# One more row in seven products, later output splits, earlier weights, and the prompt's attention work in unused columns of the score tiles: one step of a two-layer diffusion backbone

## The chip, the cores and the metric

The kernel runs on one core of one Trainium2 chip. A core has TensorE (matrix products; PE in the profile, PEld for its weight loads), VectorE (DVE), ScalarE (ACT), GpSimd (POOL) and SyncE (SP, which here only issues DMAs). Each engine works through its own queue in order and waits for the others through semaphores. Matrix products land in PSUM, which has eight banks of 512 fp32 columns in each of 128 partitions; everything else lives in SBUF. The metric is the device time of one execution in microseconds, as a median of runs.

## The reference

Two streams of tokens pass through two layers with the same weights: 128 prompt tokens, and 512 latent tokens that also see the prompt's cached keys and values. Layer 0 mixes with eight latent-compressed heads (MLA) and eight neighbourhood heads, layer 1 with grouped queries; after each mixer comes a SwiGLU FFN of width 2816. Shift, scale and gate of every sub-layer are made from a condition vector (the modulation).

```python
for l in range(DEPTH):
    sh1_s, sc1_s, g1_s, sh2_s, sc2_s, g2_s = ada_modulation(cond_lat, w_mod[l], b_mod[l])
    hs = modulate(rms_norm(xs, norm_mix[l]), sh1_s, sc1_s)
    out_s = ...          # even: q, k, v of 8 MLA heads, softmax over 512 + 128 keys; neighbourhood heads; @ w_out
    xs = xs + g1_s * out_s
    hs = modulate(rms_norm(xs, norm_ffn[l]), sh2_s, sc2_s)
    xs = xs + g2_s * swiglu(hs, w_ffn_in[l], w_ffn_out[l])
# the same for the prompt's tokens, which read only prompt tokens
def swiglu(h, w_in, w_out):
    gate, up = jnp.split(h @ w_in, 2, axis=-1)
    return (jax.nn.silu(gate) * up) @ w_out
```

## The kernel before

Activations lie with the 1024 features on partitions (8 blocks of 128) and the 640 tokens (512 latent, 128 prompt) on columns, which are worked in two halves of 320 (`HALF`). Products keep fp32 precision by splitting each operand in a high part (a ScalarE copy to fp32r) and a low part (a VectorE subtraction); `mm3` runs three matmuls for one product: high x high, high x low, low x high. Every weight block therefore costs a DMA, a ScalarE pass and a VectorE pass (`unit`, or `load` and `split`).

PSUM has two families of tiles: four banks of kind "m" (`bank`), and four more whose use changes by stage (`open_y`): single banks of kind "y", or in the attention stages two score tiles of two banks each (`bank2`, tag "s"). In a score tile of MLA, `mla_scores` uses columns 0 to 319 of each bank, and columns 320 to 511 lie unused.

Tiles and semaphores are placed by a framework that orders each engine's queue at build time, by the order in which the code writes the operations and by a model of when each becomes ready. `after(inst, fn)` and `run` add an order only: what `fn` issues on the engine of `inst` is queued behind it. `sequence(order, pieces)` runs named pieces in a written order, each behind the last matmul before it.

**MLA heads** (loop over `h` = 0 to 7; `p, r = divmod(h, 2)`, so `r` is 0 for even heads). The pieces of one head in `MLA_ORDER` are: `s0` to `s3`, the scores of four blocks of 128 latent queries against 640 keys (six matmuls into a score tile `ms`, a maximum on VectorE (L963), an exponential on ScalarE (L965), a reciprocal and a scaling on GpSimd); `q0`, `q1`, the queries of the next head; `k0`, `k1`, the keys of the next pair of heads (odd heads only); `sp`, the prompt's scores of this head; and, one head late, `t0` to `t4`, the transposes of the five blocks of probabilities with their split into `mts` (L390, L391), and `v0` to `v4`, their products with the values into `mo`. `v3` and `v4` run another head later under the names `w3` and `w4`. In the first head of a pair come also `pt` and `pv`, the transposes and value products of the prompt's probabilities of the pair before (`prompt_pair`, names mpp). All of q, k, t, mo, sp, pt and pv take banks of kind "m". The neighbourhood heads use `prompt_pair` as well, with their own banks.

**Output splits.** `rsplit` splits the attention outputs for the projection: `oNs` (neighbourhood heads, ready before the MLA heads begin) behind the fourth exponential of heads 0, 2, 4 and 5; `oMs` 0 to 2 (MLA) where the framework finds room after their pair is done, and `oMs` 3 at the end.

**Output projection** (`mixer_out`, name oa in layer 0, oc in layer 1): for each of eight output blocks n, a weight unit and 2 x 8 x 3 matmuls, then the residual (L324) and the norm's sums. From n = 1 on `beside(n - 1)` adds modulation tiles: a DMA `wm` and two VectorE products `junk` (L1630) each, whose sums are the modulation of the FFN's output and of layer 1. `early` (off in layer 0, on in layer 1) makes the weight unit of n ahead of these tiles. In the first two blocks the last operand, oMs3, comes late, so both wait with their last eighth.

**FFN rows** (`ffn`). The 22 blocks of the hidden width are rows. The first `FEW[l]` rows are made whole: gate and up, two halves, 8 blocks, `mm3`. The later rows use a form of seven products of half the depth (`product`, names fg, fd, fu) in place of eight: `seven` builds four weight tiles from the raw pair with four VectorE sums and four splits, and the activations' sums D, N, C, E are made by `add_up` during rows 0 and 1. `split` places its tiles in turn in the pools wp and fp, by the counter `turn`; the output stage's `wout` uses the same counter to choose between the pools rawp/wp and fo. The activations of most rows are spilled to memory and read back for the output stage.

Of the kernel before, what the change touches and what calls it, by code (L numbers as in the profile page):

```python
# [18 lines left out]
P = 128  # L19
D = 1024  # L20
KT = D // P
NS = 512
# [29 lines left out]
def body(ctx, tc, xT, vecs, crow, wm0, wm0g1, wm0g, wm1, wA, wNV, wNA, wMK, wMV, wOA, wGQ, wGK, wGV, wOC,  # L52
# [53 lines left out]
    def f(ap):  # L106
        return ap.bitcast(F32)
# [19 lines left out]
    def named(prefix, pieces):  # L127
        return {f"{prefix}{i}": piece for i, piece in enumerate(pieces)}
# [54 lines left out]
    def mm3(ps, a, b, h, l, st, sp, **k):  # L183
        PE.matmul(ps, a, h, start=st, stop=False, **k)
        PE.matmul(ps, a, l, start=False, stop=False, **k)
        PE.matmul(ps, b, h, start=False, stop=sp, **k)
# [196 lines left out]
        V.reciprocal(r, l)  # L383
        G.tensor_scalar(pt[:, :n], pt[:, :n], r, 0.0, ALU.mult, ALU.add)

    def pt_split(ps, n, pool, name):
        bufs = 5 if pool.name == "cp" else 3
        h = pool.tile([P, 512], F32R, tag="pth", bufs=bufs, name=name + "h")
        l = pool.tile([P, 512], F32R, tag="ptl", bufs=bufs, name=name + "l")
        S.activation(h[:, :n], ps[:, :n], AF.Copy)  # L390
        V.tensor_tensor(l[:, :n], ps[:, :n], f(h[:, :n]), ALU.subtract)  # L391
        return h, l

    def tr(out, in_):
        PE.transpose(out, in_, ident)
# [18 lines left out]
    def prompt_pair(vs, o, pool, name, sbank):  # L414

        pt = pool.tile([P, 256], F32, tag="pp", bufs=1, name=name + "p")

        def first(r, product):
            def run():
                pss = sbank(f"{name}s{r}")[:, :P]  # L420
                product(pss)
                m = tiny.tile([P, 1], F32, tag="m2", name=f"{name}m{r}")
                V.tensor_reduce(m, pss, AX.X, ALU.max, negate=True)
                l = tiny.tile([P, 1], F32, tag="l2", name=f"{name}l{r}")
                sl = pt[:, r * P:(r + 1) * P]
                S.activation(sl, pss, AF.Exp, bias=m, accum_out=l)
                softmax_tail(sl, l, f"{name}r{r}", P)
            return run

        box = []  # L430

        def trs():
            pst = bank(name + "t")
            for r in range(2):
                tr(pst[:, r * P:(r + 1) * P], pt[:, r * P:(r + 1) * P])
            box.extend(pt_split(pst, 256, pool, name + "pt"))

        def av():
            th, tl = box
            pso = bank(name + "o")  # L440
            for r in range(2):
                out = pso[:, r * P:(r + 1) * P]
# [3 lines left out]
            S.activation(t[:, :256], pso[64:128, :256], AF.Copy)  # L446
            for r in range(2):
                V.tensor_tensor(o[64 * r:64 * r + 64, NS:T], pso[0:64, r * P:(r + 1) * P], t[:, r * P:(r + 1) * P], ALU.add)

        return first, {"pt": trs, "pv": av}  # L450

# [378 lines left out]
    def k_tiles(r, p):  # L830
        return odd_keys[p % 2] if r else even_keys
# [118 lines left out]
    def mla_q(h):  # L950
        return q_pieces(h, qbank, lambda c: cp.tile([P, T], F32R, tag=f"mq{c}", bufs=2, name=f"mq{c}{h}"), lambda: tq[:, h % 2, :])

    def mla_scores(h, pts):
        r = h % 2
        ll = tiny.tile([P, 4], F32, tag="ll", bufs=4, name=f"ml{h}")

        def piece(j):
            qh, ql = mqs[h]
            pss = bank2(f"ms{h}_{j}")
            kh, kl = [t[0] for t in k_tiles(r, h // 2)]  # L960
            scores(pss, (qh[:, P * j:P * j + P], ql[:, P * j:P * j + P]), kh, kl)
            nm = tiny.tile([P, 1], F32, tag="nm", name=f"mn{h}_{j}")
            V.tensor_reduce(nm, pss[:, :, :HT], AX.XY, ALU.max, negate=True)  # L963
            pt = cp.tile([P, T], F32, tag="mp", bufs=8, name=f"mp{h}_{j}")
            exps[h, j] = S.activation(halves(pt), pss[:, :, :HT], AF.Exp, bias=nm, accum_out=ll[:, j:j + 1])  # L965
# [31 lines left out]
    for i in range(6):  # L997
        if i not in mvb and i not in BESIDE:
            mv_late(i)
    tail, oM, oNs = {}, [], []  # L1000

    MLA_ORDER = ("s0 w3 q0 w4 s1 t0 t1 pt s2 v0 t2 pv q1 v1 t3 s3 v2 t4 sp",
                 "s0 w3 q0 w4 s1 k0 t0 t1 q1 s2 v0 k1 t2 s3 v1 t3 v2 sp t4")
    late = {}
    for h in range(8):
        p, r = divmod(h, 2)
        if r == 0:
            oM.append(cp.tile([P, T], F32, tag="om", bufs=4, name=f"oM{p}"))
            pfirst, psecond = prompt_pair([mv[5][:, 2 * p + i, :] for i in range(2)], oM[p], cp, f"mpp{p}",
                                         bank)  # L1010
        pts = []
        sc = mla_scores(h, pts)
        qh, ql = mqs[h]
        pieces = named("s", sc)
        pieces["sp"] = pfirst(r, lambda pss, qh=qh, ql=ql, ks=k_tiles(r, p): mm3(pss, qh[:, NS:T], ql[:, NS:T], ks[0][1], ks[1][1], True, True))
# [654 lines left out]
    def x_again(n):  # L1670
# [10 lines left out]
    x, pend = mixer_out(wOA, oMs + oNs, [4, 5, 6, 7, 0, 1, 2, 3], x_again, mods[0], "oa", nxt, op[-1], before(op[1], op[5], (1, 1, 1, 1, 0, 0, 0)))  # L1681
    box2, nxt = next_mod("h10", gs[1][0], mods[1], SH1)
    x, pend = ffn(0, x, pend, box["m"], nxt, side, op)

# [378 lines left out]
```

## Time and profile before

| | |
|---|---|
| median of 3 runs | 1493.82 us (1493.72 to 1495.14) |
| the profiled execution | 1495.92 us |
| its span | 1494.1 us |
| TensorE / VectorE / ScalarE / GpSimd busy | 97% / 83% / 53% / 12% |
| mean granted TensorE clock | 0.994 |
| moved by DMA | 231.48 MB, 155 GB/s |

The page names engines PE, PEld, DVE, ACT, POOL and SP; L64 is a line of the kernel, and as every matmul is issued by one helper, matmuls are told apart by their tiles (out<-in). Matmuls overlap, so that a matmul of 320 columns is shown with about 0.31 us while the next begins earlier; busy time is the union of these. "[0.66 <-DVE x]" behind a row is the idle time of that engine before it and what ended it. In the windows each engine's busy time is followed by its instructions in brackets.

### The profile page before, as it was taken

The page shows a single profiled execution, that of the slowest core. Times are in us where ns is not written, and L with a number is a line of the kernel's source. Part 1 is how long each engine was busy: PE and PEld are TensorE (multiplying, and loading weights), DVE is VectorE, ACT ScalarE, POOL GpSimd, SP SyncE. Part 2 cuts the span into 40 slices and gives each one's busy share as a digit, 9 for nine tenths or more (in the row PEclk, how much of TensorE's full clock was granted, in tenths as well). Part 3 has the DMA queues.
Part 4 walks back from the last instruction along what each step waited for, and adds up shares of the span by engine and source line. Part 5 has one row for each costly group of instructions (what it writes and reads, how often), then busy time and mean ns, then how long its engine had stood idle before and what let it go on. Part 6 is the DMA issues. An engine that isn't in the chain of part 4 may idle for free.

```text
span 1494.1 us, 25843 instructions
## 1 busy us (share of the span) xinstructions
PE 1448.7 (97%) x9766; PEld 1392.5 (93%) x9766; DVE 1235.9 (83%) x2378; ACT 785.7 (53%) x1542; POOL 178.0 (12%) x272
## 2 busy tenths in 40 slices
PE   6999999999999999999999999999999999999997
PEld 4989978889899999999999999989899999999996
DVE  5877778877878888955998888888899989989976
ACT  5446677763745555541222656672665565555443
POOL 0046635420000000000000122220100000000000
PEclk9999999999999999999999999999999999999999
DMA  9643341025154554559765301115154555548561
GB/s 372 207 151 123 114 145 44 15 81 188 42 208 167 166 166 166 163 181 345 234 215 189 96 27 36 37 40 193 57 170 171 190 175 190 174 151 294 184 260 71
DMA packets 79636, 231.48 MB, mean 155 GB/s; under 512 B 8856, under 2 KB 13240, under 8 KB 79128
## 3 DMA queue, kind: packets, MB, share of 16 engines
q1 hardware_dynamic: 77152, 225.43, 44.2%
q10 hardware_dynamic: 1944, 3.48, 0.7%
q8 instruction: 76, 1.25, 0.3%
q0 software_dynamic: 416, 0.93, 0.2%
q14 instruction: 48, 0.39, 0.1%
HBM read 193.15 MB, written 36.66 MB: 154 GB/s over the span
## 4 chain that ended last, share of the span: by engine, by line
PE 77%; DVE 10%; ACT 6%; DMA 4%; issue 2%; POOL 0%; DVEq 0%; ACTq 0%; SPq 0%; POOLq 0%
PE fg L64 19%; PE fd L64 9%; PE fgo L64 5%; PE fu L64 4%; PE gq L64 3%; PE fdo L64 3%; PE fo L64 2%; DVE junk L1630 2%; PE gs L64 2%; PE go L64 2%; PE nk L64 2%; PE nq L64 2%; PE fuo L64 1%; PE gt L68 1%; PE mod L64 1%
## 5 line engine op out<-in xcount | busy, mean ns | idle before, releaser
L1630 DVE SCALAR_TENSOR_TENSOR junk<-wm,cb 128x1024 bf16<-128x1024 f32 x88 | 107.3, 1219 | 1.8 <-DMA wm<-in_wm 1.2
L64 PE MATMUL gq<-h10h,wgq 128*128 128x320 f32 x256 | 65.8, 316 | 0.0
L261 POOL TENSOR_SCALAR h10h<-h10t,gs,mods 128x320 fp32r<-128x320 f32 x4 | 3.1, 786 | 438.2 <-DVE h10t L255 435.9
L1370 ACT ACTIVATE wY<-s 128x1024 fp32r<-128x1024 f32 x37 | 39.2, 1060 | 27.7 <-PE fg L64 24.0
L1898 POOL TENSOR_TENSOR xr<-xw,fn1rs 128x320 f32<-128x320 f32 x2 | 1.7, 866 | 416.9 <-ACT fn1rs L229 416.9
L1370 ACT ACTIVATE wZ<-s 128x1024 fp32r<-128x1024 f32 x37 | 39.1, 1057 | 18.8 <-PE fd L64 16.5
L1479 DVE TENSOR_TENSOR sg<-up,sg 128x640 f32<-128x640 f32 x37 | 30.5, 823 | 20.7 <-ACT sg L1478 19.6
L1371 DVE TENSOR_TENSOR wZ<-s,wZ 128x1024 fp32r<-128x1024 f32 x37 | 45.2, 1222 | 2.8 <-ACT wZ L1370 0.2
L64 PEld LDWEIGHTS gq<-h10h,wgq 128*128 128x128 f32 x256 | 44.9, 189 | 0.6
L1371 DVE TENSOR_TENSOR wY<-s,wY 128x1024 fp32r<-128x1024 f32 x37 | 45.1, 1219 | 0.3
L1478 ACT ACTIVATE sg<-fg 128x320 f32<-128x320 f32 x37 | 16.2, 438 | 48.7 <-PE fg L64 48.7
L64 PE MATMUL fg<-h01q,wgu 128*128 128x320 f32 x192 | 40.3, 316 | 0.9 <-ACT h01q L298 0.5
L1500 ACT ACTIVATE p<-fd 128x320 f32<-128x320 f32 x37 | 16.2, 438 | 46.9 <-PE fd L64 46.9
L64 PE MATMUL gq<-h10l,wgq 128*128 128x320 f32 x128 | 39.4, 308 | 0.0
L1835 ACT ACTIVATE gp<-gs,gb,rq 128x640 f32<-128x640 f32 (+1 forms) x40 | 31.8, 796 | 13.2 <-DVE gb L1834 11.8
L64 PE MATMUL fg<-h11q,wX 128*128 128x320 f32 x228 | 36.7, 309 | 0.0
L64 PE MATMUL fu<-h11q,wX 128*128 128x320 f32 x228 | 36.6, 309 | 0.0
L64 PE MATMUL fd<-h11q,wZ 128*128 128x320 f32 x228 | 36.6, 309 | 0.0
L64 PE MATMUL fg<-h11E,wW 128*128 128x320 f32 x228 | 36.5, 309 | 0.0
L64 PE MATMUL fg<-h11N,wZ 128*128 128x320 f32 x228 | 36.5, 309 | 0.0
L64 PE MATMUL fd<-h11D,wY 128*128 128x320 f32 x228 | 36.4, 308 | 0.0
L64 PE MATMUL fg<-h11C,wY 128*128 128x320 f32 x228 | 36.4, 308 | 0.0
(3425 smaller groups left out, 5331.1 us busy)
## 6 DMA issues: line engine op xcount, KB each, us to landing
wm<-in_wm SPq DMA_DIRECT2D x48, 512.0 KB, 4.3
mraw<-in_wm SPq DMA_DIRECT2D x8, 1024.0 KB, 13.2
mraw<-in_wm SPq DMA_DIRECT2D x16, 512.0 KB, 4.0
wmv<-in_wm0g SPq DMA_DIRECT2D x8, 512.0 KB, 4.3
wm<-in_wm0g SPq DMA_DIRECT2D x8, 512.0 KB, 3.5
ruo<-in_wFO SPq DMA_DIRECT2D x8, 512.0 KB, 4.7
rgo<-in_wFO SPq DMA_DIRECT2D x8, 512.0 KB, 5.9
x<-in_xT SPq DMA_DIRECT2D x8, 320.0 KB, 5.4
```

The lines of the kernel that those rows point to most:

```text
L64: cls.last = nc.tensor.matmul(*a, **k)
L68: cls.last = nc.tensor.transpose(*a, **k)
L261: G.tensor_scalar(h[:, c0:c1], t, self.gsl[:, k, 0:1], self.ml[:, self.sh + k, 0:1], ALU.mult, ALU.add)
L1370: S.activation(h, src, AF.Copy)
L1371: V.tensor_tensor(w_, src, f(h), ALU.subtract)
L1478: last = S.activation(sg[:, 0:HT], g[:, :HT], AF.Silu, scale=-1.0)
L1479: V.tensor_tensor(sg, up, sg, ALU.mult)
L1500: S.activation(p5, b5[:, :HT], AF.Copy)
L1630: V.scalar_tensor_tensor(junk, raw, 1.0, cb[:, c, :], ALU.mult, ALU.mult, accum_out=mods[l][:, j0 + i, c:c + 1])
L1835: gexp[h, j] = S.activation(dst, src, AF.Exp, bias=nb, scale=rq[:, j:j + 1], accum_out=ll[:, j:j + 1])
L1898: G.tensor_tensor(x[k][:, c0:c1], root[1][k], nrm.rs[:, c0:c1], ALU.mult)
```

## The change

Five edits:

1. `FEW` of layer 0 goes from 4 to 3: row 3 of its FFN is made in seven products.
2. `oNs` 3 is split behind the third exponential of head 7 and `oMs` 0 to 2 behind its fourth, on ScalarE's queue.
3. The output projection of layer 0 is called with `early`.
4. In `MLA_ORDER` of even heads `s1` goes ahead of `w4`, and `sp`, `pt` and `pv` leave the order.
5. `sp`, `pt` and `pv` of the MLA heads are run inside a score piece, right behind its six matmuls and ahead of its maximum, into columns 320 to 447 of the score tile's two banks: in even heads `pt` in `s1`, `sp` in `s2` and `pv` in `s3`, in odd heads `sp` in `s3`. Head 7's `sp` and the last pair's `pt` and `pv` stay as they were, with banks of kind "m".

```diff
-    def pt_split(ps, n, pool, name):
+    def pt_split(ps, n, pool, name, shape=None):
...
-        S.activation(h[:, :n], ps[:, :n], AF.Copy)
-        V.tensor_tensor(l[:, :n], ps[:, :n], f(h[:, :n]), ALU.subtract)
+        shape = shape or (lambda t: t[:, :n])
+        ps = shape(ps) if len(ps.shape) == 2 else ps
+        S.activation(shape(h), ps, AF.Copy)
+        V.tensor_tensor(shape(l), ps, f(shape(h)), ALU.subtract)
...
+        def both(t):
+            return t[:, :256].rearrange("p (a b) -> p a b", a=2)
+
         def first(r, product):
-            def run():
-                pss = sbank(f"{name}s{r}")[:, :P]
+            def run(spare=None):
+                pss = sbank(f"{name}s{r}")[:, :P] if spare is None else spare[:, 0]
...
-        def trs():
-            pst = bank(name + "t")
+        def trs(spare=None):
+            pst = both(bank(name + "t")) if spare is None else spare
             for r in range(2):
-                tr(pst[:, r * P:(r + 1) * P], pt[:, r * P:(r + 1) * P])
-            box.extend(pt_split(pst, 256, pool, name + "pt"))
+                tr(pst[:, r], pt[:, r * P:(r + 1) * P])
+            box.extend(pt_split(pst, 256, pool, name + "pt", both))
...
-        def av():
+        def av(spare=None):
             th, tl = box
-            pso = bank(name + "o")
+            pso = both(bank(name + "o")) if spare is None else spare
...
-    def mla_scores(h, pts):
+    def mla_scores(h, pts, beside):
...
             scores(pss, (qh[:, P * j:P * j + P], ql[:, P * j:P * j + P]), kh, kl)
+            if j in beside:
+                beside[j](pss[:, :, HT:HT + P])
...
-    MLA_ORDER = ("s0 w3 q0 w4 s1 t0 t1 pt s2 v0 t2 pv q1 v1 t3 s3 v2 t4 sp",
+    MLA_ORDER = ("s0 w3 q0 s1 w4 t0 t1 s2 v0 t2 q1 v1 t3 s3 v2 t4",
                  "s0 w3 q0 w4 s1 k0 t0 t1 q1 s2 v0 k1 t2 s3 v1 t3 v2 sp t4")
...
-        sc = mla_scores(h, pts)
         qh, ql = mqs[h]
-        pieces = named("s", sc)
-        pieces["sp"] = pfirst(r, lambda pss, ...: mm3(...))
+        beside = {1: tail.pop("pt"), 3: tail.pop("pv")} if h and r == 0 else {}
+        pieces = named("s", mla_scores(h, pts, beside))
+        (pieces if h == 7 else beside)["sp" if h == 7 else 3 - (r == 0)] = pfirst(r, lambda pss, ...: mm3(...))
...
-        if h in (0, 2, 4, 5):
+        if h in (0, 2, 4):
             oNs.append(after(exps[h, 3], lambda: rsplit(oN[len(oNs)], f"oNs{len(oNs)}")))
-    oMs = [rsplit(oM[p], f"oMs{p}") for p in range(3)]
+    oNs.append(after(exps[7, 2], lambda: rsplit(oN[3], "oNs3")))
+    oMs = [after(exps[7, 3], lambda: rsplit(oM[p], f"oMs{p}")) for p in range(3)]
...
-    FEW = 4, 3
+    FEW = 3, 3
...
-    x, pend = mixer_out(wOA, oMs + oNs, ..., before(op[1], op[5], (1, 1, 1, 1, 0, 0, 0)))
+    x, pend = mixer_out(wOA, oMs + oNs, ..., before(op[1], op[5], (1, 1, 1, 1, 0, 0, 0)), True)
```

More of the change, by code (lines that the diff above doesn't have):

```diff
@@ L430, in prompt_pair @@
         box = []
-        def trs():
-            pst = bank(name + "t")
+        def trs(spare=None):
+            pst = both(bank(name + "t")) if spare is None else spare
             for r in range(2):
-                tr(pst[:, r * P:(r + 1) * P], pt[:, r * P:(r + 1) * P])
-            box.extend(pt_split(pst, 256, pool, name + "pt"))
-        def av():
+                tr(pst[:, r], pt[:, r * P:(r + 1) * P])
+            box.extend(pt_split(pst, 256, pool, name + "pt", both))
+        def av(spare=None):
             th, tl = box
-            pso = bank(name + "o")
+            pso = both(bank(name + "o")) if spare is None else spare
             for r in range(2):
-                out = pso[:, r * P:(r + 1) * P]
+                out = pso[:, r]
                 PE.matmul(out, vs[r], th[:, r * P:(r + 1) * P], start=True, stop=False)
@@ L445, in av @@
             t = pool.tile([64, 512], F32, tag="hs", bufs=1, name=name + "h")
-            S.activation(t[:, :256], pso[64:128, :256], AF.Copy)
+            S.activation(both(t), pso[64:128], AF.Copy)
             for r in range(2):
-                V.tensor_tensor(o[64 * r:64 * r + 64, NS:T], pso[0:64, r * P:(r + 1) * P], t[:, r * P:(r + 1) * P], ALU.add)
+                V.tensor_tensor(o[64 * r:64 * r + 64, NS:T], pso[0:64, r], t[:, r * P:(r + 1) * P], ALU.add)
         return first, {"pt": trs, "pv": av}
@@ L1011, in body @@
         pts = []
-        sc = mla_scores(h, pts)
         qh, ql = mqs[h]
-        pieces = named("s", sc)
-        pieces["sp"] = pfirst(r, lambda pss, qh=qh, ql=ql, ks=k_tiles(r, p): mm3(pss, qh[:, NS:T], ql[:, NS:T], ks[0][1], ks[1][1], True, True))
+        beside = {1: tail.pop("pt"), 3: tail.pop("pv")} if h and r == 0 else {}
+        pieces = named("s", mla_scores(h, pts, beside))
+        (pieces if h == 7 else beside)["sp" if h == 7 else 3 - (r == 0)] = pfirst(r, lambda pss, qh=qh, ql=ql, ks=k_tiles(r, p): mm3(pss, qh[:, NS:T], ql[:, NS:T], ks[0][1], ks[1][1], True, True))
         if h == 0:
@@ L1680, in body @@
                             (0, 1, 1, 1, 2, 2, 2, 2, 3, 3, 3, 3, 3, 2, 2, 2)[i])
-    x, pend = mixer_out(wOA, oMs + oNs, [4, 5, 6, 7, 0, 1, 2, 3], x_again, mods[0], "oa", nxt, op[-1], before(op[1], op[5], (1, 1, 1, 1, 0, 0, 0)))
+    x, pend = mixer_out(wOA, oMs + oNs, [4, 5, 6, 7, 0, 1, 2, 3], x_again, mods[0], "oa", nxt, op[-1], before(op[1], op[5], (1, 1, 1, 1, 0, 0, 0)), True)
     box2, nxt = next_mod("h10", gs[1][0], mods[1], SH1)
```

## The prediction

> **What bounds the kernel now.** I read the page first: the share of each engine, then the chain that ended last.
>
> ```profile
> span 1494.1 us, 25843 instructions
> PE 1448.7 (97%) x9766; PEld 1392.5 (93%) x9766; DVE 1235.9 (83%) x2378; ACT 785.7 (53%) x1542; POOL 178.0 (12%) x272
> PE 77%; DVE 10%; ACT 6%; DMA 4%; issue 2%; POOL 0%; DVEq 0%; ACTq 0%; SPq 0%; POOLq 0%
> ```
>
> TensorE is busy for 97% of the span, so a part is worth the matmuls that it removes or the TensorE waits that it ends. I therefore asked for busy times of the stages that the diff touches, with two stages of layer 1 beside them that are written in the form the diff gives to layer 0.
>
> ```profile
> core 0: us, PE busy (x) PEld busy (x) DVE busy (x) ACT busy (x) POOL busy (x), PEclk, DMA share, GB/s
> 226.00:320.00 94.00, 87.60 (x567) 78.33 (x565) 82.75 (x174) 74.75 (x172) 46.80 (x55) 1.00 0.09 29
> 320.00:331.00 11.00, 10.94 (x72) 9.68 (x71) 6.88 (x17) 5.49 (x11) 0.69 (x2) 1.00 0.24 97
> 331.00:369.00 38.00, 37.20 (x252) 36.70 (x251) 27.86 (x53) 11.67 (x18) 2.40 (x1) 1.00 0.62 211
> 1001.00:1039.00 38.00, 38.00 (x256) 36.96 (x255) 29.23 (x54) 13.31 (x24) 0.00 (x0) 1.00 0.49 172
> 400.00:428.00 28.00, 27.23 (x182) 26.68 (x183) 21.26 (x42) 16.14 (x31) 0.00 (x0) 1.00 0.60 212
> 428.00:442.00 14.00, 13.06 (x88) 12.68 (x88) 13.60 (x19) 6.86 (x10) 0.00 (x0) 1.00 0.55 194
> 1083.00:1111.00 28.00, 27.85 (x188) 27.30 (x187) 27.78 (x56) 17.93 (x37) 0.00 (x0) 1.00 0.53 173
> 500.00:525.00 25.00, 25.00 (x172) 25.00 (x172) 22.27 (x35) 13.31 (x21) 0.00 (x0) 1.00 0.53 179
> ```
>
> 226 to 320 us is the latent heads (MLA), 320 to 331 their tail, 331 to 369 layer 0's output projection, 1001 to 1039 that of layer 1; 400 to 442 are the first FFN rows of layer 0, 1083 to 1111 rows 1 and 2 of layer 1, and 500 to 525 the steady rows. In the heads TensorE is idle for 94.00 - 87.60 = 6.4 us, and VectorE is busy for 82.75 of the 94 us (88%): it is nearly a second bound. The granted clock is 1.00 in every row, so no part of this is a matter of the clock. Third, what TensorE waited for in these stages (us in total, times, longest):
>
> ```profile
> PE mt L68 <- DVE kTql L844: 1.4, 2, 0.7
> PE mo L64 <- DVE mts_4l L391: 1.2, 1, 1.2
> PE ms L64 <- ACT mp L965: 1.1, 2, 0.6
> PE mpp1o L64 <- ACT mts_2h L390: 0.7, 1, 0.7
> PE mpp0o L64 <- DVE mts_1l L391: 0.7, 1, 0.7
> ...
> PE mt L68 <- DVE kTp L844: 0.5, 1, 0.5
> PE mpp2o L64 <- DVE mpp2ptl L391: 0.3, 1, 0.3
> ```
>
> ```profile
> PE fu_3a L64 <- DVE wgu L174: 0.9, 1, 0.9
> PE oa3a L64 <- DVE oaw L174: 0.5, 1, 0.5
> ...
> PE fu_2a L64 <- ACT wgu L173: 0.4, 1, 0.4
> ```
>
> **Row of seven (FEW 4 to 3).** In the whole form a row is 2 outputs x 2 halves x 8 blocks x 3 = 96 matmuls of 320 columns; in the form of seven products it is 7 x 4 x 3 = 84. In the steady rows 172 of these take 25.00 us, 0.145 us each: 12 x 0.145 = 1.74 us off TensorE's own work. The wait of fu_3a (0.9) is for the second weight of whole row 3, a tile that is no longer made. In its place row 3 has four sums and four splits on VectorE. Layer 1 already starts its rows of seven after three whole ones: there VectorE is as good as full (27.78 of 28) and TensorE still runs 27.85 of 28, against 27.23 of 28 and then 13.06 of 14 in layer 0. So I let the 0.9 go and keep fu_2a's 0.4. Bounds: -1.74 - 0.9 - 0.4 = -3.0, and above, row 3 waits for its operands for about as long as 428 to 442 idles, 14.00 - 13.06 = 0.94, twice over: -1.74 + 1.9 = +0.2. I take **-2.6 us**.
>
> One side effect: split and wout share the counter turn, and one more row of seven adds three splits, so each single wout tile of the output stage of this FFN changes between the pools rawp and fo. TensorE waits there once today:
>
> ```profile
> PE fo_6a L64 <- DVE wo L1547: 0.9, 1, 0.9
> ```
>
> This wait can go or come again elsewhere: bounds -0.9 and +0.9, and with as many tiles in either pool I take **0**.
>
> **Weights ahead of modulation (early=True).** No instruction is added; in each step from the second on the weight unit is issued ahead of the modulation tile, its DMA on SP's queue ahead of the tile's, its split on VectorE ahead of the two products (junk). Now the split of unit 3 stands behind them:
>
> ```profile
> 347.98 1.22 DVE L174 TENSOR_TENSOR oaw<-oaw3r,oaw 128x1024 fp32r<-128x1024 f32 x1
> ```
>
> oa3a waited 0.5 for it. Layer 1's projection, which has this order, runs 38.00 of 38; layer 0's 37.20: 0.8 us at most. What is queued behind is the modulation products, which nobody needs before this FFN's output; VectorE has 38.00 - 27.86 = 10 us free to make them. If that cover were gone, the norm's sums would wait for one product behind them, 1.2 us. Bounds -0.8 and +0.4; I take **-0.8 us**.
>
> **Late output splits.** Four splits (oNs3, oMs0 to oMs2) leave the busy heads and are queued on ScalarE behind the last two exponentials of head 7. Where three of them stand now:
>
> ```profile
> 296.87 1.31 DVE L462 TENSOR_TENSOR oNs3l<-oN,oNs3h 128x640 fp32r<-128x640 f32 x1
> 299.90 0.81 DVE L462 TENSOR_TENSOR oMs0l<-oM,oMs0h 128x640 fp32r<-128x640 f32 x1
> 306.60 1.40 DVE L462 TENSOR_TENSOR oMs1l<-oM,oMs1h 128x640 fp32r<-128x640 f32 x1 [0.24 <-ACT oMs1h L461]
> 311.26 0.50 PE L64 MATMUL mo<-mts_4l,mv 128*128 128x512 f32 x1 [1.16 <-DVE mts_4l L391]
> ```
>
> The last of these rows is the largest wait of the stage: VectorE comes late to mts_4l, with oMs1l among what it does before. I let its 1.2 us go. In the tail the four need 4 x 0.81 = 3.2 us of VectorE, which idles there for 11.00 - 6.88 = 4.1 us, and 5.5 us are free on ScalarE. Queued behind them are head 7's splits (mts), for which TensorE waits; it has products of oNs0 to oNs2 to fill with. Cost 0, bounds 0 and +1.2 (one such wait coming back there). Together **-1.2 us**.
>
> **Prompt's work in the score tiles.** The same instructions run; 7 score products (sp), 3 pairs of transposes (pt) and 3 of values (pv) no longer take a bank of the four of kind m. With them go the waits that stand right behind them: t4's for kTql and kTp (1.4 + 0.5) and pv's (0.7 + 0.7 + 0.3), 3.6 us. What it adds is time in which a score tile is held; there are two. The operations that now hold it:
>
> ```profile
> 257.06 0.42 PE L64 MATMUL mpp1s<-kTp,mqh 128*128 128x128 f32 x2
> 258.83 0.28 DVE L423 TENSOR_REDUCE mpp1m<-mpp1s 128x1 f32<-128x128 f32 x1
> 259.83 0.35 ACT L426 ACTIVATE mpp1p<-mpp1s,mpp1m 128x128 f32<-128x128 f32 x1
> 251.55 0.40 ACT L390 ACTIVATE mpp0pth<-mpp0t 128x256 fp32r<-128x256 f32 x1
> 252.69 0.41 DVE L391 TENSOR_TENSOR mpp0ptl<-mpp0t,mpp0pth 128x256 fp32r<-128x256 f32 x1
> 304.65 0.38 ACT L446 ACTIVATE mpp2h<-mpp2o 64x256 f32<-64x256 f32 x1 [0.27 <-PE mpp2o L64]
> 305.20 0.57 DVE L448 TENSOR_TENSOR oM<-mpp2o,mpp2h 64x128 f32<-64x128 f32 x2
> ```
>
> Do they run beside the tile's own maximum and exponential, or ahead of them? A place where two engines read two halves of one bank:
>
> ```profile
> 860.15 0.38 ACT L1760 ACTIVATE gvh<-gvp 128x256 fp32r<-128x256 f32 x1 [1.47 <-DVE gvl L1761]
> ```
>
> ScalarE waited here 1.47 us for VectorE's read of the same bank's other half, in the order in which the kernel writes them. So I take it that the main maximum stands behind ScalarE's read beside it: a tile is held longer by 0.4 (its matmuls) + 0.28 + 0.35 = 1.0 us with sp, by 0.2 + 0.40 + 0.41 = 1.0 with pt (two transposes, taken as half of the four matmuls' 0.4), and by 0.4 + 0.38 + 0.57 = 1.35 with pv. [...] Were that not so, a tile would be held longer by the matmuls alone, nothing would be given back below, and the forecast would be 2.2 us lower.
>
> How much room a tile has, at the tightest place, the fourth block of head 2, whose tile head 3's second block takes:
>
> ```profile
> 255.96 0.46 PE L64 MATMUL ms<-kTh,mql 128*128 128x320 f32 x2
> 257.51 0.81 DVE L963 TENSOR_REDUCE mn<-ms 128x1 f32<-128x640 f32 x1
> 258.42 0.79 ACT L965 ACTIVATE mp<-ms,mn 128x640 f32<-128x640 f32 x1 [0.41 <-DVE mn L963]
> 260.17 0.30 PE L64 MATMUL ms<-kToh,mqh 128*128 128x320 f32 x1
> ```
>
> From 259.21 to 260.17 there are 0.96 us. With pv beside it 1.35 are added: 0.4 short, in three heads 1.2 us. In the odd heads sp is added, and the next use comes sooner, since s1 now stands ahead of w4 (two matmuls) and the waits behind sp are gone; no row gives that, so I put 0 to 0.7 for each of heads 0, 1, 3 and 5 and take 0.25: 1.0 us. Sum -3.6 + 2.2 = **-1.4 us**, with bounds -3.6 and, at 13 places of 1.0 us, +9.4.
>
> **The sum.** -2.6 - 0.8 - 1.2 - 1.4 = -6.0 us. The profiled execution took 1495.92 us, 1.8 beside its span of 1494.1; the median of the runs is 1493.82, 2.1 lower, and I carry that difference over: 1489.9 profiled, **1487.8 us** as a median. A measurement of this kernel can tell about 0.2% from no change, 3.0 us.
>
> **Rivals.**
> 1. The score tile becomes the wait. Every one of the 13 places adds 1.0 us or more to a tile's life, and the chain crosses from VectorE to ScalarE and back once more in queues that are 88% and 74.75 / 94 = 80% busy. It decides from the point where the room is under the addition, and 0.96 us at one place says that this is near. If TensorE waits 1.0 us at each: -6.0 + (13.0 - 2.2) = +4.8, 1498.6 us. Against: most tiles are not the tightest. [...]
> 2. VectorE bounds the heads. At 88% a TensorE wait that is ended only meets VectorE's next late operation: the 4.8 us of the heads come to nothing, and the flipped pools cost 0.9. -2.6 - 0.8 + 0.9 = -2.5, 1491.3 us. Against: the splits that leave are VectorE's own work.
> 3. Row 3 comes too soon: with 13.60 of 14 us busy in 428 to 442, VectorE makes row 3's and row 4's operands back to back, and TensorE waits 1.9 us. That makes this part +0.2 in place of -2.6: 1490.6, and with the flipped pools' 0.9 1491.5 us. Layer 1's 27.85 of 28 speaks against it.
>
> **How the numbers follow.** The forecast has 0.68, its own range being 1483 (all idle time of the heads, 6.4, with 3.0, 0.8 and 0.9 gained, is 11.1 less, 1482.7) to 1490.8. Rivals 2 and 3 lie within 3.0 us of no change: 0.10 and 0.06. Rival 1 has 0.16 and is slower by more than that at full price; a third of its price would bring the kernel back to 1491.4. So faster 0.68, same 0.16, slower 0.16. The range reaches from 1483 into rival 1 at two thirds of its price (-6.0 + 7.2 = +1.2, 1495.0), to 1496 with a piece for the unknown ends of row 3: it leaves out 0.16 to 0.2.
>
> **What would show it.** Row of seven: twelve matmuls fewer between the end of the projection and the FFN's output, no fu_3a, TensorE at 14 of 14 in the stretch after row 2. Weights: the split of oaw unit 3 right behind its ScalarE half, no wait of oa3a, 38.00 of 38. Late splits: oMs0l to oMs2l after head 7's last exponential, no 1.16 us ahead of mo<-mts_4l. Score tiles: no wait of mt for kTql or of mpp0o and mpp1o, and in their place waits of ms for mp (now 1.1 us in all). I am wrong if the ms waits sum to more than 4.8 us, if VectorE rises over 95% in the heads with TensorE still idle for 6 us, or if the output stage of the FFN gains a new wait of several us.

## The result, and the profile after

The changed kernel takes 1488.58 us (median of 13 runs, 1487.11 to 1493.2) against 1494.11 us of the kernel before on the same chip (13 runs, 1491.67 to 1498.65). The ratio is 0.9961 with a 95% interval of 0.9951 to 0.9970, that is 4.5 to 7.3 us less, 5.8 us in the middle. The forecast was 1487.8 us, 6.0 us less. The sum is right; its terms are not, as the stages show.

The page of the changed kernel:

```profile
span 1486.6 us, 25813 instructions
PE 1444.4 (97%) x9754; PEld 1389.2 (93%) x9754; DVE 1238.6 (83%) x2386; ACT 789.1 (53%) x1547; POOL 179.6 (12%) x272
...
PE 83%; DVE 8%; ACT 5%; issue 2%; DMA 2%; DVEq 0%; ACTq 0%; SPq 0%
```

Twelve matmuls are gone (9766 to 9754), and VectorE's and DMA's shares of the chain have shrunk (10 to 8% and 4 to 2%). Where the time went is read from the stages, each cut at its first matmul on TensorE: heads and tail (from the first `ms` to `oa2a`), the rest of the output projection (to the first gate product `fg`), the FFN's rows (to `fo_0a`), the output stage (to layer 1's first product). The windows of the kernel before, and below them those of the changed kernel; the columns are the stretch, its length and the busy time of PE, PEld, DVE, ACT and POOL with their instructions, the granted clock, DMA share and GB/s:

```profile
225.73:339.85 114.12, 107.66 (x698) 97.12 (x696) 93.82 (x202) 80.98 (x183) 47.49 (x56) 1.00 0.16 56
339.85:383.93 44.08, 43.28 (x292) 42.63 (x291) 32.65 (x62) 16.41 (x29) 3.32 (x3) 1.00 0.39 132
383.93:666.34 282.41, 280.14 (x1888) 276.69 (x1887) 237.41 (x366) 149.21 (x246) 1.08 (x2) 1.00 0.47 158
666.34:826.57 160.23, 157.90 (x1073) 156.98 (x1071) 129.80 (x234) 37.17 (x56) 1.99 (x3) 1.00 0.72 244
```

```profile
225.13:336.99 111.86, 107.24 (x697) 96.19 (x696) 91.77 (x198) 80.90 (x183) 49.42 (x56) 1.00 0.15 53
336.99:379.77 42.78, 42.78 (x292) 42.62 (x291) 33.51 (x65) 16.39 (x29) 3.33 (x3) 1.00 0.45 148
379.77:660.46 280.69, 278.26 (x1876) 274.98 (x1875) 245.61 (x378) 151.54 (x250) 1.07 (x2) 1.00 0.48 163
660.46:818.63 158.17, 157.36 (x1072) 156.94 (x1071) 125.43 (x228) 38.50 (x57) 2.27 (x2) 1.00 0.69 241
```

The four stages give 2.26, 1.30, 1.72 and 2.06 us less, 7.34 together in this pair of profiles; as the table below shows, the last of them scatters from profile to profile. The forecast had 2.6 (late splits 1.2, score tiles 1.4), 0.8, 2.6 and 0. What TensorE waited for in the heads and tail of the changed kernel (us in total, times, longest):

```profile
PE mo L64 <- DVE mts_4l L393: 1.6, 3, 1.0
PE ms L64 <- ACT mp L972: 1.5, 2, 1.0
PE mo L64 <- DVE mts_3l L393: 0.6, 3, 0.2
PE mo L64 <- DVE mts_0l L393: 0.5, 2, 0.3
...
```

The waits of `mt` for kTql and kTp and of `mpp0o` to `mpp2o` are gone, as forecast. The waits of `ms` for the score tile, which the forecast let grow by 2.2 us, grew from 1.1 to 1.5. In their place stand waits of `mo` for `mts`, VectorE's half of a split.

### The profile page after: what moved, and what is told of

Read it like the earlier page. It is cut to its first block, busy times and chain, and to the rows that moved or that the text cites. A ratio compares the mean times of both kernels' runs of the same rounds, so it can differ in the third digit from the quotient of the medians.

```text
span 1486.6 us, 25813 instructions
## 1 busy us (share of the span) xinstructions
PE 1444.4 (97%) x9754; PEld 1389.2 (93%) x9754; DVE 1238.6 (83%) x2386; ACT 789.1 (53%) x1547; POOL 179.6 (12%) x272
## 4 chain that ended last, share of the span: by engine, by line
PE 83%; DVE 8%; ACT 5%; issue 2%; DMA 2%; DVEq 0%; ACTq 0%; SPq 0%
PE fg L64 18%; PE fd L64 9%; PE fgo L64 5%; PE fo L64 5%; PE fu L64 4%; PE gq L64 3%; PE fdo L64 3%; PE gs L64 2%; PE go L64 2%; PE nk L64 2%; PE nq L64 2%; PE fuo L64 1%; PE gt L68 1%; PE mod L64 1%; PE gvp L64 1%
## 5 line engine op out<-in xcount | busy, mean ns | idle before, releaser
L64 PE MATMUL fg<-h01N,wZ 128*128 128x320 f32 x228 | 36.6, 309 | 1.4 <-ACT p L1506 1.4
L64 PE MATMUL fg<-h01E,wW 128*128 128x320 f32 x228 | 36.6, 310 | 0.8 <-DVE g L1518 0.8
L64 PE MATMUL fg<-h01q,wX 128*128 128x320 f32 x228 | 36.7, 309 | 0.0
L64 PE MATMUL fd<-h01q,wZ 128*128 128x320 f32 x228 | 36.6, 309 | 0.0
```

What stands on the lines that cost most here:

```text
L64: cls.last = nc.tensor.matmul(*a, **k)
```

## The experiments

Each kernel below was profiled, so that the stages can be compared. A stage that a kernel leaves alone repeats to about 0.1 us in the first two columns, and much less well in the last two. The expectations cut the first column in two at `oa0a`: 93.36 us of heads and 20.75 of tail before, 91.30 and 20.56 in the changed kernel. All times in us:

| kernel | heads and tail | projection | rows | output stage |
|---|---|---|---|---|
| before | 114.12 | 44.08 | 282.41 | 160.23 |
| changed, first profile | 111.86 | 42.78 | 280.69 | 158.17 |
| e1 row of seven alone | 114.16 | 44.08 | 281.96 | 158.13 |
| e2 early weights alone | 114.13 | 42.78 | 282.54 | 158.93 |
| e3 late splits alone | 112.78 | 47.21 | 285.60 | 158.42 |
| e4 score tiles alone | 113.94 | 44.07 | 283.90 | 159.00 |
| e5 pools flipped alone | 114.13 | 44.08 | 282.30 | 158.83 |
| e6 changed, again | 111.86 | 42.79 | 280.95 | 161.16 |
| e7 main reads first | 115.11 | 42.78 | 282.75 | 158.07 |
| e8 p1 first in row 3 | 111.85 | 42.79 | 279.55 | 161.23 |
| e9 row of seven, pools as before | 114.13 | 44.07 | 280.83 | 159.13 |
| e10 p1 first, one modulation tile earlier | 111.88 | 42.78 | 281.17 | 157.75 |
| e11 as e8, timed | 111.89 | 42.79 | 280.86 | 158.07 |
| e12 changed, timed | 111.89 | 42.78 | 280.86 | 157.93 |

**One edit at a time, on the kernel before.** The row of seven:

```diff
-    FEW = 4, 3
+    FEW = 3, 3
```

> The kernel before with row 3 of layer 0's FFN made as a row of seven, nothing else. Theory A (parts add up by stage): the FFN rows, from the first gate product to the first output product, take 282.41 - 1.72 = 280.7 us, with the new wait of fg for p of about 1.4 us behind row 3's first product and no wait of fu_3a; the output stage, which gets the other pool for each single wout tile, goes from 160.23 to 158.2 us, with no waits of fo_6a and fn0p. Sum about -3.8 us. Rival B (the output stage's gain comes from another edit, by the moment at which the stage starts): rows 280.7, output stage still 160.2, sum -1.7 us. Rival C (row 3's wait for p comes only because the rows start sooner or with other weights resident): the rows take 279.8, as was forecast (-2.6).

Output stage 158.13: theory A. The rows, 281.96, lie 1.3 above the 280.7 of A and B and rule out C: `fu_3a` no longer waits, but TensorE waits 1.8 us for p (p1, ScalarE's copy of a row's first product, out of the bank into which the third product goes on). They also lose 0.5 to a wait for a later row's g (VectorE's sum of a row's last product in that bank and p5), of which only e11 has another (0.3).

The weights ahead of modulation:

```diff
-    ... before(op[1], op[5], (1, 1, 1, 1, 0, 0, 0)))
+    ... before(op[1], op[5], (1, 1, 1, 1, 0, 0, 0)), True)
```

> The kernel before with weights ahead of modulation in layer 0's projection, nothing else. Theory A: the projection, from oa2a's first product to the FFN's first gate product, takes 44.08 - 1.30 = 42.8 us: oa3a's 0.5 us goes, and the rest at the end of the stage; rows and output stage as before (282.4 and 160.2). Rival B (0.5 of the 1.30 is the forecast's wait, and 0.8 comes from the late output splits, which leave less to do behind the tail): 43.5 us. If the output stage goes to 158.2 here, its gain is the phase and not the pools.

Theory A to the hundredth: 42.78, so all of the projection's 1.30 us belongs to this edit. Its output stage, 158.93, is 1.3 below the kernel before, though nothing there was touched: a wait of `fn0p` that the kernel before has in its profile is missing here.

```profile
PE fn0p L64 <- DVE fn0acc L208: 1.4, 1, 1.4
```

The late output splits:

```diff
-        if h in (0, 2, 4, 5):
+        if h in (0, 2, 4):
...
-    oMs = [rsplit(oM[p], f"oMs{p}") for p in range(3)]
+    oNs.append(after(exps[7, 2], lambda: rsplit(oN[3], "oNs3")))
+    oMs = [after(exps[7, 3], lambda: rsplit(oM[p], f"oMs{p}")) for p in range(3)]
```

> The kernel before with the four late output splits, nothing else. Theory A (the forecast's step): heads and tail, from the first score product to oa0a, 112.36 - 1.2 = 111.2 us, the 1.16 us wait ahead of mo<-mts_4l of head 7 gone. Rival B (that wait comes from VectorE's whole queue and stays, as in the changed kernel, where it still is 1.05 us): 112.3 us, at most 0.2 less, because work only moves from the heads into the tail. Projection, rows and output stage as before.

Heads and tail 112.78, 1.34 less: theory A, by its own wait. All that is left of waits of `mo` in the heads is one of 0.2:

```profile
PE mo L64 <- DVE mts_0l L391: 0.2, 1, 0.2
```

But the projection takes 3.13 us more, so in this profile, the only one of this kernel, the edit alone costs 1.8 us over the two stages. TensorE's wait there, and the windows behind it (columns as above, the clock third from the end):

```profile
PE oa3a L64 <- DVE oaw L174: 2.1, 1, 2.1
```

```profile
345.00:348.00 3.00, 0.73 (x4) 0.30 (x2) 3.00 (x7) 0.87 (x2) 0.00 (x0) 1.00 0.47 184
348.00:349.00 1.00, 0.90 (x3) 0.90 (x4) 1.00 (x2) 0.00 (x0) 0.00 (x0) 0.60 0.00 0
349.00:350.00 1.00, 1.00 (x5) 1.00 (x5) 1.00 (x3) 0.00 (x0) 0.00 (x0) 0.50 0.77 193
350.00:351.00 1.00, 1.00 (x6) 1.00 (x5) 1.00 (x2) 0.00 (x0) 0.00 (x0) 0.50 0.79 315
351.00:352.00 1.00, 1.00 (x7) 1.00 (x6) 1.00 (x3) 0.00 (x0) 0.00 (x0) 0.69 0.48 94
```

The wait of oa3a, 0.5 us before, is 2.1: TensorE reaches the projection sooner (112.78 us after the heads' first product, 114.12 before), the modulation tiles come no sooner (VectorE's first product of one starts after 109.1 us, 108.7 before), and the split of unit 3 stands behind their products on VectorE (it starts after 122.5 us, 122.3 before). Then TensorE runs for four us at about half its clock, 0.40 + 0.50 + 0.50 + 0.31 = 1.7 us lost. The growth of the wait (1.6) and the clock (1.7 by these windows) account for the 3.13. With early weights beside it, as in the changed kernel, the projection is 42.78 and nothing of this is left: edit 3 takes the cost of edit 2 away. The rows of this kernel are 3.2 us longer than before as well, though nothing there was touched: `fu_3a` waits 2.2 us in place of 0.9, and the clock falls behind that wait too (0.62 over the next four us). In e4, below, `fu_3a` also waits 2.2, the clock stays at 1.00, and the rows are 1.5 longer.

The score tiles, with their order of pieces, alone (edits 4 and 5 of the change, the rest as before):

```diff
-    MLA_ORDER = ("s0 w3 q0 w4 s1 t0 t1 pt s2 v0 t2 pv q1 v1 t3 s3 v2 t4 sp",
+    MLA_ORDER = ("s0 w3 q0 s1 w4 t0 t1 s2 v0 t2 q1 v1 t3 s3 v2 t4",
...
+            if j in beside:
+                beside[j](pss[:, :, HT:HT + P])
```

> The kernel before with the prompt's work in unused columns of the score tiles' banks and its order of pieces, nothing else. Theory A: heads and tail take 112.36 - 2.2 = 110.1 us, all of what the changed kernel gains there: waits of mt for kTql and kTp and of mpp0o, mpp1o, mpp2o gone (3.6), about 1.4 given back as waits of ms for mp and of mo for mts. Rival B (the score tiles gain only together with the late splits, because VectorE bounds the heads): 111.3 us or more. Rows and output stage as before.

Rival B, and further than it went: 113.94, 0.18 less than before. All 3.6 us of waits behind sp, pt and pv are gone, and the rest has come back here:

```profile
PE mo L64 <- DVE mts_4l L393: 1.8, 3, 1.2
PE ms L64 <- ACT mp L972: 1.5, 2, 1.0
PE mo L64 <- DVE mts_0l L393: 1.4, 4, 0.5
PE mo L64 <- DVE mts_3l L393: 1.0, 4, 0.3
PE mt L68 <- POOL mp L384: 0.5, 1, 0.5
```

4.2 us of waits of `mo` for VectorE's mts (1.7 before), only 0.4 more for the tile, and 0.5 for GpSimd's scaling. With the late splits, which take VectorE's work out of the heads, the same edit is worth 112.78 - 111.86 = 0.92 us. The two are worth more together (2.26) than one by one (1.34 + 0.18).

**Which read goes first in a score tile.** Changed kernel, with the prompt's reads queued behind the tile's own:

```diff
-                beside[j](pss[:, :, HT:HT + P])
+                rest = beside[j](pss[:, :, HT:HT + P])     # the products alone
...
             softmax_tail(pt, ll[:, j:j + 1], f"mr{h}_{j}", T)
+            if rest:
+                rest()                                     # the prompt's reads
```

> The changed kernel, but the prompt's reads in a score tile (maximum and exponential of sp, split of pt, sums of pv) are queued behind the tile's own maximum, exponential and scaling, and not ahead of them. Theory A (the forecast's: the tile's own maximum stands behind ScalarE's read beside it, so that the probabilities come late, and the splits mts of the next head with them): the small waits of mo for mts_0, mts_3 and mts_4 (2.7 us in all) and of ms for mp (1.5) shrink by half or more, heads 91.30 - 2 = about 89.3 us. Rival B (VectorE and ScalarE do the same work in the same time, and the small waits are those of a full VectorE, whichever of the two reads comes first): 91.3 us within 0.5. Rival C: pt's and pv's splits now come too late for the products behind them, 92 to 93 us, with new waits of mpp0o to mpp2o.

All three expectations missed: the heads take 94.53, and with the tail 115.11, slower than the changed kernel by 3.25 us and than the kernel before by 1.0. Not the products behind pt and pv wait, but the score tile:

```profile
PE ms L64 <- ACT mp L986: 2.5, 2, 2.0
PE ms L64 <- DVE oM L468: 1.6, 2, 0.9
...
PE ms L64 <- ACT oNs1h L481: 0.7, 1, 0.7
```

4.8 us of waits of `ms` against 1.5. So the forecast's first rival is real, in the other order. In 1.6 of the 4.8 us it is the prompt's sums `oM` that end a tile's life, and the next block's scores wait for them. The longest wait, 2.0 us after head 0's last block, is put down to ScalarE's exponential mp; the prompt's own exponential of that head is queued right behind it, and which of the two held the tile the profile does not tell. The order of the change costs less, though the tile's own maximum does come after ScalarE's read of the spare columns there. On the changed kernel's timeline, head 1's fourth block, and then a row of head 0's third:

```profile
243.30 0.27 DVE L428 TENSOR_REDUCE mpp0m<-ms 128x1 f32<-128x128 f32 x1
243.60 0.37 ACT L431 ACTIVATE mpp0p<-ms,mpp0m 128x128 f32<-128x128 f32 x1
244.35 0.82 DVE L970 TENSOR_REDUCE mn<-ms 128x1 f32<-128x640 f32 x1
```

```profile
230.76 0.16 DVE L383 RECIPROCAL mpp0r0r<-mpp0l 128x1 f32<-128x1 f32 x1 [0.59 <-ACT mpp0p L431]
```

The maximum mn comes 1.05 us after mpp0m began, as the forecast held (1.0), but VectorE fills that time with other rows of its queue; that mn itself waited for ScalarE's read is not shown. In head 0, where there are fewer such rows, it stands idle for 0.59 us until ScalarE's exponential of the prompt is done (the reciprocals run on VectorE), and TensorE's wait for the tile there grows from 0.60 to 0.97: that is the 0.4.

**The wait in row 3.** In the changed kernel, ScalarE's rows ahead of p1 and what TensorE makes of it:

```profile
428.68 1.05 ACT L1378 ACTIVATE wX<-wu_4r 128x1024 fp32r<-128x1024 f32 x1
429.63 1.05 ACT L1378 ACTIVATE wZ<-s 128x1024 fp32r<-128x1024 f32 x1
430.57 0.72 ACT L1438 ACTIVATE hd_0h<-sg 128x640 fp32r<-128x640 f32 x1
431.20 0.42 ACT L1506 ACTIVATE p<-fg 128x320 f32<-128x320 f32 x1
...
431.68 1.00 PE L64 MATMUL fg<-h01N,wZ 128*128 128x320 f32 x5 [1.38 <-ACT p L1506]
```

p1 stands behind two splits of row 4, which TensorE needs only after row 3, some ten us later. The edit puts it first:

```diff
-            wX, wW, wY, wZ = seven(ru, rg, f"{l}_{fb}", fp, split)
+            wX, wW, wY, wZ = after(copied if l == 0 and fb == few + 1 else None, lambda: seven(...))
...
-            S.activation(p1, g[:, :HT], AF.Copy)
+            copied = S.activation(p1, g[:, :HT], AF.Copy)
```

> The changed kernel, but the ScalarE work that makes row 4's weight tiles is queued behind the copy p1 of row 3. Theory A (TensorE's wait of 1.4 to 1.9 us behind row 3's first products is p1's place on ScalarE, behind three splits of row 4 that wait for sums of late weights): the wait goes, rows 280.69 - 1.5 = about 279.2 us. Rival B (row 4's tiles are then late themselves): the wait comes again one row later, rows 280.7 or more.

```profile
428.77 0.74 ACT L1438 ACTIVATE hd_0h<-sg 128x640 fp32r<-128x640 f32 x1 [1.94 <-DVE sg L1472]
429.41 0.42 ACT L1506 ACTIVATE p<-fg 128x320 f32<-128x320 f32 x1
429.73 1.05 ACT L1378 ACTIVATE wX<-wu_4r 128x1024 fp32r<-128x1024 f32 x1
```

The wait is gone and the rows take 279.55, 1.1 to 1.4 less: theory A. The second profile of the same kernel (e11) has the wait gone too, but rows of 280.86: what it gained is lost again in four waits of 0.3 to 0.5 us, three of them 80 to 200 us further on. That gives rival B's number, but not its mechanism, a wait of row 4. What the edit is worth lies between 0 and 1.4 us.

**The output stage.** It moved by 1.2 to 1.8 us in three kernels that never touched it (e2 to e4); most of that is the wait of `fn0p`, which they do not have. Two kernels changed the pools and the row apart from each other (one extra count of `turn`, on the kernel before and on the kernel with the row of seven):

```diff
         close(job)
+        turn[0] += 1
         fs.close()
```

> The kernel before with one extra count of the turn ahead of layer 0's output stage, nothing else: each single wout tile of that stage takes the other pool, and every queue up to there is that of before. Theory A (the wait of fo_6a for wo at the seventh tile belongs to the pool that the tile takes): no wait of fo_6a, as in the two kernels with the row of seven (0 of 2), against 1.09 us beyond the usual step in the four kernels without it; output stage about 1.1 us below a kernel with the same other waits. Rival B (the wait goes because the stage is entered at another moment): fo_6a waits 1.09 us again. Up to the output stage this is also a second look at the kernel before: heads 93.36, tail 20.75, projection 44.08, rows 282.41 us; a row-3 wait of fu_3a near 1.1 us says that the 2.35 us of the late-splits and score-tile kernels is theirs, one near 2.35 that it is the landing of row 4's weights, which moves from run to run. The same for the 1.5 us ahead of the last norm's sum, seen in the kernel before alone.

> The kernel before with row 3 as a row of seven and one extra count of the turn, so that each single wout tile keeps the pool that it has in the kernel before. Up to here fo_6a waited 1.08 us in all five kernels with row 3 whole (also in the one whose pools alone were flipped) and in none of the four with row 3 in seven products. Theory A (the place of the split of wo_60 in VectorE's queue, which the build sets by when it thinks a tile is ready, and not the pool alone): the wait depends on row and pool together; it may come or not here. Theory B (the row of seven alone removes it, whatever the pools): no wait of fo_6a here. Theory C (the two flips must meet): 1.08 us again. Rows as in the kernel with the row of seven alone, 281.96 us, with 1.5 to 2.1 us of wait for p behind row 3's first products.

Waits of the output stage, first with the pools flipped alone, then with the row of seven and the pools as before:

```profile
PE fo_6a L64 <- DVE wo L1548: 0.9, 1, 0.9
...
```

```profile
PE fn0p L64 <- DVE fn0acc L208: 1.3, 1, 1.3
```

fo_6a waits in all five kernels with row 3 whole, the flipped one among them, and in none of the nine profiles with the row of seven. Theory B: the row removes this 1.1 us, and the pools alone have nothing to do with it. (The rows of e9, 280.83, are 1.1 below the 281.96 expected: its wait for p is 1.5, and e1's wait for a later g is not there.) One row of before and one of after show how the wait goes:

```profile
716.69 0.82 DVE L1547 TENSOR_TENSOR wo<-wo_60r,wo 128x640 fp32r<-128x640 f32 x1
```

```profile
706.07 0.82 DVE L1555 TENSOR_TENSOR wo<-wo_60r,wo 128x640 fp32r<-128x640 f32 x1
```

Before, VectorE's half of wo_60 comes 4.7 us after ScalarE's (711.25 to 711.99), queued behind modulation products and residuals, one of which waits 1.30 us for TensorE; after, 1.7 us after it (703.61 to 704.35). In the five kernels with row 3 whole this distance is 4.1 to 4.9 us, in the nine others 0.3 to 1.8. So the row of seven gives VectorE's queue another order here; why the build chose it no run shows. The wait of fn0p (1.3 to 1.4) is in two of the five kernels with the pools of before (before and e9) and in none of the others; why was not settled.

e5 is the kernel before up to this stage, and repeats it: 282.30 in the rows, and fu_3a's step is 1.0 longer than usual, against 1.1.

**How much a stage scatters.** The changed kernel a second time, unchanged:

> The changed kernel, a second profile, to tell what a stage's time scatters by. If stages repeat: heads 91.30, tail 20.56, projection 42.78, rows 280.69, output stage 158.17 us, each within 0.1 us but the rows, where the wait of fg for p behind row 3's first products was 1.5 us here and 1.9 us in the kernel with the row of seven alone; a rival, that these differences come from the other edits, gives 280.7 again to 0.1 us.

Heads and projection repeat, the rows come to 280.95 with 1.8 lost behind row 3's first products, and the output stage takes 161.16, 3.0 us more. VectorE's row ahead of the last row's g, in the first and the second profile:

```profile
659.51 1.23 DVE L1638 SCALAR_TENSOR_TENSOR junk<-wm,cb 128x1024 bf16<-128x1024 f32 x1 [0.69 <-DMA wm<-in_wm]
```

```profile
660.62 1.23 DVE L1638 SCALAR_TENSOR_TENSOR junk<-wm,cb 128x1024 bf16<-128x1024 f32 x1 [2.29 <-DMA wm<-in_wm]
```

A modulation product waits at the head of VectorE's queue for its DMA, g stands behind it, and TensorE's wait for g goes from 0.8 to 2.3 us. Then, in the second profile, the clock (third column from the end) falls:

```profile
661.00:664.00 3.00, 0.74 (x6) 0.48 (x5) 3.00 (x7) 0.33 (x2) 0.00 (x0) 1.00 1.03 387
664.00:668.00 4.00, 4.00 (x18) 4.00 (x19) 1.49 (x2) 1.58 (x3) 0.00 (x0) 0.60 0.93 354
```

1.5 us of wait and 4 x 0.40 = 1.6 us of clock make the 3.0. An attempt to move the product away (with e8's edit, the tile of row 20 taken in row 18):

```diff
-                            lambda kind, i: int(i > 4 and i % 3 > 0 or i == 21) if kind == "fb" else
+                            lambda kind, i: int(i > 4 and i % 3 > 0 and i != 20 or i in (18, 21)) if kind == "fb" else
```

> The changed kernel with p1 of row 3 ahead of row 4's ScalarE work, and with the modulation tile of row 20 taken two rows earlier (row 18), so that no product of it stands ahead of the last row's g on VectorE. Theory A (the wait of fg for g at the start of the output stage, 0.97 and 2.42 us in two runs of the changed kernel, is two modulation products that wait for their DMA on VectorE ahead of g): output stage 158.17 - 0.97 = 157.2 us, rows 279.5. Rival B (the products only move and hold VectorE in rows 18 to 20): rows 280.5 or more, output stage 157.2. Rival C (the tile of row 21 takes the place ahead of g): output stage 158.2 to 161.2 as before.

Rival B, and partly C: the output stage 157.75 with 0.4 left of the wait, and the rows 281.17, with 1.2 us of new waits of `fg` for u. Nothing gained.

**p1 first, timed.**

> The changed kernel with p1 of row 3 ahead of row 4's ScalarE work, timed. By its stage (rows 279.55 against 280.69 and 280.95 us) it should be 1.1 to 1.4 us faster than the changed kernel beside it, about 0.1%: a ratio to the kernel before near 0.9953 if the changed kernel's is 0.9961. Rival: the waits that move with the landing of DMAs (0.9 to 2.5 us at the start of the output stage) hide it, and the two ratios cannot be told apart.

> The changed kernel, timed beside it on the same chip: ratio to the kernel before 0.9951 to 0.9970 as on record. In the profile, rows 280.7 to 281.0 us; the output stage 158.2 or 161.2 us, by whether the last row's g waits 0.97 or 2.42 us for the modulation products ahead of it.

With p1 first: 1487.01 us (6 runs, 1483.66 to 1488.21), ratio to the kernel before 0.9940, interval 0.9925 to 0.9955. The changed kernel beside it: 1488.92 us (6 runs, 1486.28 to 1493.13), 0.9961, interval 0.9945 to 0.9976. Its median is 1.9 us lower, but the intervals overlap, and in the profiled executions the rows take 280.86 us in both: it cannot be called faster than the changed kernel. In e12's profile g is waited for 0.6 us, less than in either profile expected, and the output stage is 157.93.

## Why the prediction was right, and where it was not

**Row of seven: -2.6 forecast, -1.5 to -1.7 in the changed kernel.** The 1.74 us of twelve matmuls are there. The step that failed is "I let the 0.9 go": the wait of fu_3a went, and an idle time of 1.4 to 1.7 us ahead of row 3's third product, which waits for p, took its place. (fu_2a's wait, kept at 0.4, came down to 0.15.) Rival 3 named this (row 3's and row 4's operands back to back, 1.9 us) with a chance of 0.06; the wait came at 0.7 to 0.9 of its price. Both waits hang on the landing of a weight, but not of the same one. fu_3a's hangs on row 4's. ScalarE's split of it in the kernel before and in e4:

```profile
427.24 1.06 ACT L1370 ACTIVATE wX<-wu_4r 128x1024 fp32r<-128x1024 f32 x1 [2.75 <-DMA wu_4r<-in_wFI]
```

```profile
427.75 1.06 ACT L1377 ACTIVATE wX<-wu_4r 128x1024 fp32r<-128x1024 f32 x1 [4.24 <-DMA wu_4r<-in_wFI]
```

Against the start of the rows (383.93 and 382.95) that is 43.3 and 44.8 us; fu_3a's wait is 0.9 and 2.2. The wait for p hangs on row 3's own second weight, now that row 3 is the first row of seven. VectorE's first sum of it in the changed kernel and in e7:

```profile
419.64 0.69 DVE L1187 TENSOR_TENSOR s<-wg_3r 128x512 f32<-128x512 f32 x1 [3.13 <-DMA wg_3r<-in_wFI]
```

```profile
421.46 0.69 DVE L1203 TENSOR_TENSOR s<-wg_3r 128x512 f32<-128x512 f32 x1 [3.66 <-DMA wg_3r<-in_wFI]
```

That is 39.9 and 40.4 us after the start of the rows (379.77 and 381.06), and the waits for p are 1.4 and 1.9; e1, e6, e9 and e12 lie between, and in all six the wait is the time of this row less 38.5. Row 4's weight does not set it: in e12 that one lands 1.3 us sooner after the start of the rows than in the first profile of the changed kernel, and p is waited for 0.2 us longer. From this landing on VectorE works almost without a gap (11.49 of 11.56 us in the changed kernel) through row 3's and row 4's sums and splits until p is there, as rival 3 had it; ScalarE's splits of row 4 wait for these sums, and p1 stands behind them. The rows of layer 1, on which the forecast leaned, did not show such a wait (TensorE was busy for 27.85 of 28 us).

**The flipped pools: 0 forecast, within 0.9; measured -2.06, +0.93 and -2.30 in three profiles of the changed kernel.** Outside its bounds on both sides. The mechanism was wrong (e5, e9): the certain part, 1.1 us, comes with the row of seven and another order of VectorE's queue, whatever the pools. The rest is a wait for g that moves with a DMA's landing, and with it the clock, and the wait of fn0p in the one profile of the kernel before. Against e2 to e5, which keep row 3 whole and have no wait of fn0p (158.4 to 159.0), the changed kernel's output stage is 0.3 to 1.1 us shorter in two profiles and 2.2 to 2.7 longer in one. A bound taken from one wait of one execution was too narrow.

**Weights ahead of modulation: -0.8 forecast, -1.30.** The mechanism is as told: oa3a's wait is gone and TensorE works 42.78 of 42.78 us. The term was mis-sized, because idle time is not all that a wait costs: the same 292 matmuls also took 0.50 us less of busy time. The first matmul behind oa3a's wait of 0.5 us is shown with 0.41 us, the next ones with 0.31.

**Late output splits: -1.2 forecast, -1.34 alone, by the wait named.** In the changed kernel that wait is still there, behind other work:

```profile
306.59 0.57 DVE L453 TENSOR_TENSOR oM<-ms,mpp2h 64x128 f32<-64x128 f32 x2
307.18 0.82 DVE L970 TENSOR_REDUCE mn<-ms 128x1 f32<-128x640 f32 x1
307.92 0.68 DVE L393 TENSOR_TENSOR mts_4l<-mt,mts_4h 128x512 fp32r<-128x512 f32 x1
...
308.66 0.49 PE L64 MATMUL mo<-mts_4l,mv 128*128 128x512 f32 x1 [1.05 <-DVE mts_4l L393]
```

pv's sums and the maximum behind them now stand ahead of mts_4l. Beside the score tiles the gain of this edit, 113.94 - 111.86 = 2.08 us, shows in other waits of the last two heads instead: 2.7 us of waits for mts in all (4.2 without it), and none for GpSimd's scaling. Its cost in the projection without edit 3 was not foreseen.

**Prompt's work in the score tiles: -1.4 forecast, -0.92 beside the late splits, -0.18 alone.** The 3.6 us left as forecast; 2.7 of it came back beside the late splits and 3.4 alone, where the forecast had 2.2. The step that failed is where: "how much room a tile has" was worked out for the tile, and the tile had room (0.4 more). VectorE had not, which was rival 2, with a chance of 0.10: a wait that is ended there met VectorE's next late split. Rival 2 came true in part only: it left the heads nothing, and VectorE is busy for 78.88 of the changed heads' 91.30 us (86%), so it is the order of its queue that comes late and not its sum. Rival 1 came true only when the prompt's reads went last.

So the total was right in part by luck: the heads and the rows gave 1.2 us less than forecast, the projection 0.5 more, and the output stage, forecast at nothing, made up the rest by a mechanism that was not foreseen and by waits that move from run to run.

## What to carry to other kernels

Ask of each removed wait which operation of the late engine's queue is next: the waits for fu_3a (0.9 us), kTql (1.4) and mpp0o to mpp2o (1.7) went as told, and waits behind a later row of another engine's queue (1.4 for p, 2.7 for mts) took their place. Test edits one by one and together: the late splits alone cost more in the projection (3.13 us) than they gave in the heads (1.34), and the score tiles gave almost nothing alone (0.18); each paid only beside another. VectorE's wait for a modulation tile, with g behind it in the queue, moved from 0.69 to 2.29 us between two profiles of the changed kernel, and TensorE's wait for g from 0.8 to 2.3; bound such a stage from several profiles.

## What the runs showed of the hardware

**A wait of about 2 us cost twice in five cases of seven.** Of seven TensorE waits between 1.9 and 2.3 us in these stages, five (oa3a and fu_3a in e3, g in e6 and e8, p in e7) were followed by some four us with a mean granted clock of 0.57 to 0.69 (0.50 at the lowest). Behind the other two (fu_3a 2.2 in e4, ms 2.0 in e7) and behind p's wait of 1.8 in e1 the clock stayed at 1.00. The measured 1.9 to 2.3 us is the length to plan with. Why five of seven did it and two did not was not settled.

**A wait cost more than its idle time.** For fu_3a of the kernel before the profile shows 0.94 us idle, and the step between the two matmuls is 1.10 longer than usual; for fo_6a 0.9 and 1.09, for oa3a 0.5 and 0.67.
